# A hybrid attention block on one core: the weights' tiles begin 32 bytes lower, at a multiple of 256

## The chip, the cores and the metric

The kernel runs on one core of a Trainium2 chip, in one launch. Its time is the device time of one execution in microseconds (us), and a kernel's time is the median of its runs. A profile is one further execution, recorded by the hardware profiler; its times are the start and length of each instruction and of each DMA packet.

A core has a matrix engine (TensorE, "PE" in the profile, with its weight loads listed as "PEld"), a vector engine (VectorE, "DVE"), a scalar engine (ScalarE, "ACT"), GpSimd ("POOL"), and a sync engine ("SP") that issues DMAs. Operands lie in SBUF, a memory of 128 partitions; an address in this document is the byte within a partition, the same for all 128. A matrix product has a *stationary* operand, which a weight load puts into the array, and a *moving* operand, whose columns are streamed past it; in the kernel's calls these are `lhsT` and `rhs`.

## The reference, cut to what matters

Sixteen learned tokens are put before a sequence of 512 tokens of width 1024. One layer follows: a norm, one wide input projection (six blocks of 1024 columns), two branches of attention with eight heads each, gates, an output projection, and a gated feed-forward part (1024 to 2816 to 1024). All is float32.

```python
xn = rmsnorm(h, norm_mix_g[l])
proj = xn @ w_in[l]
sb_q, sb_k, sb_v, df_q, df_k, df_v = jnp.split(proj, splits, axis=-1)
...
y_sb = o_sb @ w_br_sb[l]
y_df = o_df @ w_br_df[l]
gates = jax.nn.sigmoid(xn @ w_gate[l] + b_gate[l]).reshape(B, L_pad, 2, D)
merged = gates[:, :, 0] * y_sb + gates[:, :, 1] * y_df
h = h + merged @ w_out[l]
hn = rmsnorm(h, norm_ffn_g[l])
h = h + (jax.nn.silu(hn @ w_ffn_gate[l]) * (hn @ w_ffn_up[l])) @ w_ffn_down[l]
```

## The kernel before, in words

**Products in three parts.** Each float32 operand is split into a rounded part (`h`, type float32r) and the remainder (`l`). `mm3` (lines 293 to 298) makes one product out of three matrix instructions per slice of 128 rows: line 296 takes h times h, line 297 the second pairing, line 298 the third. So nearly all of PE's work is on these three lines, 128 rows deep, with 256, 264 or 512 moving columns.

**The weights' way.** `stream` is the list of all 512 KB weight pieces in the order of use. `stage_one` (line 210 issues the DMA, on SP's queue) loads a piece from DRAM into a tile `wst`. `split` then makes `wh` on ACT (a copy with rounding, line 78) and `wl` on DVE (the difference, line 81). PE reads `wh` and `wl`. The tiles `wst` (three buffers), `wh` and `wl` (four each) are all those of the pool `wpool`, each 4,096 bytes per partition: 45,056 bytes in all. SP loads a buffer again when DVE has read it; ACT and DVE fill a buffer of `wh` or `wl` again when PE is done with it.

**Who is moving and who is stationary.** In the projections, the gates and the two feed-forward products (`proj`, `product`) a slice of `wh` or `wl` is stationary and the activations move: the normed input `xT` (tiles `xT_h`, `xT_l`, whole 512 tokens or the two halves `H1`, `H2` of 264), later the hidden state `hT` in the same places (halves `T1`, `T2` of 256 tokens), the attention output (`o_h`, `o_l`), and sums of blocks (`tA`, `tB`, and `t1`, `t2`, `t4`). In the output projection (`out_steps`) and the feed-forward's last product (`step`) it is the other way round: the activations (`mg_h`, `mg_l`, `t...`, and `da`) are stationary and `wh`, `wl` move, 512 columns at a time; only the last phase of `step` moves some in pieces of 256.

**Order.** The head of the program is written out by hand in order; behind it the units of one head's projection are woven into the attention of the one before. Each engine works through its own queue in program order and waits by semaphores.

**Where tiles lie.** Pools are laid out one after the other. First come the constants (pool `const`), with `cn` (two columns used, taken from a wider tile), `eps_c` and `var_max` as the last of them, all of these rounded up to 32 bytes; then `wpool`; then `xtp`, whose first tile is `pad_x`, used by nothing, followed by `xT_h` and `xT_l`; then the rest. In the program of the kernel before, the first `wst` begins at byte 20,000, the first `wh` at 32,288 and `xT_h` at 65,248. Within a block of 256 bytes these begin at 32, 32 and 224. All tiles of `wpool` begin at 32 (45,056 and 4,096 are multiples of 256), and so does each slice of 512 bytes of them. `xT` and `hT` begin at 224 in each of their rows; the second half `H2` of `xT` begins 1,056 bytes on, at 0; the 512 tokens behind the 16 learned ones begin 64 bytes on, at 32. The tiles `o_h`, `o_l`, `mg_h`, `mg_l` and `da` begin at 32, and `t1`, `t2`, `t4` at 224.

Of the kernel before, what the change touches and what calls it, by code (L numbers as in the profile page):

```python
# [9 lines left out]
F32 = mybir.dt.float32  # L10
# [6 lines left out]
P = 128  # L17
# [24 lines left out]
def block_kernel(ctx: ExitStack, tc: tile.TileContext, x, meta, norm_mix_g, w_in, w_gate, b_gate,  # L42
# [8 lines left out]
    const = ctx.enter_context(tc.tile_pool(name="const", bufs=1))  # L51
    wpool = ctx.enter_context(tc.tile_pool(name="wpool", bufs=4))
    xtp = ctx.enter_context(tc.tile_pool(name="xtp", bufs=1))
# [276 lines left out]

    xv = x[0].rearrange("(t p) d -> p t d", p=P)

    xtp.tile([P, 48], F32, name="pad_x")
    xT_h = xtp.tile([P, KT, XP], F32R, tag="xT_h", name="xT_h")
    xT_l = xtp.tile([P, KT, XP], F32R, tag="xT_l", name="xT_l")
    xT = (xT_h, xT_l)
# [473 lines left out]
        return [first, rest]  # L810

    g_sub = const.tile([P, 1], F32, name="g_sub")
    cn = const.tile([P, 16], F32, name="cn")[:, 0:2]
    csc, nlam = cn[:, 0:1], cn[:, 1:2]
    eps_c = const.tile([P, 1], F32, name="eps_c")
    var_max = const.tile([P, 1], F32, name="var_max")
# [176 lines left out]
    for br in range(2):  # L993
        name, head = (("y_sb", sb_head), ("y_df", df_head))[br]
# [536 lines left out]
```

## Time and profile before

| What | Value |
|---|---|
| median of 3 runs | 933.06 us (931.36 to 1141.8) |
| the profiled execution | 930.84 us, of which the span of the program's instructions is 929.1 us |
| PE | 916.9 us busy, 6,009 matrix instructions |
| DVE, ACT, POOL | 733.4, 583.6 and 168.6 us busy |
| DMA | 158.41 MB, 171 GB/s on average |

Busy time is time in which at least one instruction of the engine was in progress. Matrix instructions are pipelined: one begins before the one ahead of it has ended, so that the length shown for one (276 ns, say) is longer than the step from one start to the next. What PE delivers is read from the starts. A line of the kind "L296 PE MATMUL mm<-xT_h,wh" gives the code line, the engine, the operation, the tile that is written, and the moving and the stationary tile in this order.

### The profile page before, as it was taken

What the parts mean: (1) busy time and instruction counts of PE and PEld (TensorE: products, weight loads), DVE (VectorE), ACT (ScalarE), POOL (GpSimd) and SP (SyncE); (2) the same over time, 40 slices, a digit from 0 to 9 for tenths busy, and PEclk for the clock granted to TensorE, in tenths of its full rate; (3) what the DMA queues carried; (4) which work ended last, traced back from release to release, by engine and by line L of the source; (5) the groups of instructions that cost most, each with busy time, mean ns of one, the idle gap of its engine ahead of it and who ended that gap; (6) DMA issues with size and microseconds to landing.
All of it is one profiled execution on the core that took longest, in us unless ns stands there. A gap on an engine that the chain in (4) does not pass through costs nothing.

```text
span 929.1 us, 16027 instructions
## 1 busy us (share of the span) xinstructions
PE 916.9 (99%) x6009; PEld 835.0 (90%) x6010; DVE 733.4 (79%) x1412; ACT 583.6 (63%) x1102; POOL 168.6 (18%) x199
## 2 busy tenths in 40 slices
PE   8999999999999999999999999999999999999997
PEld 5999999998999899998988888899999999988886
DVE  7988877776677766976663787899888889799975
ACT  7665676676666666666665555775555655576554
POOL 4000121222333343344512000001100000000013
PEclk9999999999999999999999999999999999999999
DMA  8525788778777978799987774427754343276642
GB/s 253 143 72 161 167 185 199 177 167 252 192 191 175 220 168 182 183 208 192 194 207 175 220 262 159 126 79 182 172 129 120 93 135 92 92 271 194 191 148 91
DMA packets 155823, 158.41 MB, mean 171 GB/s; under 512 B 6465, under 2 KB 117218, under 8 KB 155746
## 3 DMA queue, kind: packets, MB, share of 16 engines
q1 hardware_dynamic: 132690, 101.61, 36.1%
q0 software_dynamic: 22896, 55.72, 29.3%
q8 instruction: 47, 0.77, 0.3%
q14 instruction: 30, 0.25, 0.1%
q10 hardware_dynamic: 160, 0.07, 0.0%
HBM read 133.64 MB, written 50.86 MB: 199 GB/s over the span
## 4 chain that ended last, share of the span: by engine, by line
PE 94%; DVE 2%; ACT 2%; issue 1%; DMA 0%; ACTq 0%; DVEq 0%
PE mm L296 22%; PE mm L297 22%; PE mm L298 22%; PE z L296 7%; PE z L298 7%; PE z L297 7%; PE z L563 2%; PE z L696 1%; PE z L695 1%; PE tr L537 1%; DVE wl L81 1%; PE z L584 1%; DMA wst<-in_w_ffn_up_dram 0%; DVE hres L1200 0%; PE mm L855 0%
## 5 line engine op out<-in xcount | busy, mean ns | idle before, releaser
L296 PE MATMUL mm<-xT_h,wh 128*128 128x264 f32 (+2 forms) x656 | 213.6, 326 | 0.5 <-ACT xT_h L898 0.5
L297 PE MATMUL mm<-xT_l,wh 128*128 128x264 f32 (+2 forms) x656 | 213.4, 325 | 0.5
L298 PE MATMUL mm<-xT_h,wl 128*128 128x264 f32 (+2 forms) x656 | 212.6, 324 | 0.0
L78 ACT CAST wh<-wst 128x1024 fp32r<-128x1024 f32 (+1 forms) x147 | 141.4, 966 | 77.4 <-PE mm L297 55.5
L81 DVE TENSOR_TENSOR wl<-wst,wh 128x1024 fp32r<-128x1024 f32 (+1 forms) x147 | 163.3, 1116 | 31.2 <-ACT wh L78 30.9
L297 PEld LDWEIGHTS mm<-xT_l,wh 128*128 128x128 f32 x656 | 123.4, 188 | 10.3 <-DVE xT_l L899 1.3
L298 PEld LDWEIGHTS mm<-xT_h,wl 128*128 128x128 f32 x656 | 123.5, 188 | 10.0
L296 PEld LDWEIGHTS mm<-xT_h,wh 128*128 128x128 f32 x656 | 123.4, 188 | 10.0 <-ACT xT_h L898 0.9
L296 PE MATMUL mm<-hT_h,wh 128*128 128x256 f32 x304 | 83.8, 277 | 0.9 <-ACT hT_h L1157 0.8
L298 PE MATMUL mm<-hT_h,wl 128*128 128x256 f32 x304 | 83.9, 277 | 0.0
L297 PE MATMUL mm<-hT_l,wh 128*128 128x256 f32 x304 | 83.8, 276 | 0.0
L296 PEld LDWEIGHTS mm<-hT_h,wh 128*128 128x128 f32 x304 | 56.9, 188 | 1.3 <-ACT hT_h L1157 1.0
L699 DVE CUSTOM_DVE_ANT_0 pr<-z,bias 128x144 f32<-128x144 f32 (+3 forms) x64 | 30.9, 502 | 34.0 <-PE z L696 31.8
L297 PEld LDWEIGHTS mm<-hT_l,wh 128*128 128x128 f32 x304 | 57.0, 188 | 0.0
L298 PEld LDWEIGHTS mm<-hT_h,wl 128*128 128x128 f32 x304 | 57.0, 188 | 0.0
L296 PE MATMUL mm<-o_h,wh 128*128 128x512 f32 x128 | 52.4, 410 | 0.0
L296 PE MATMUL z<-wh,da 128*128 128x512 f32 (+1 forms) x132 | 50.3, 381 | 0.0
L297 PE MATMUL z<-wl,da 128*128 128x512 f32 (+1 forms) x132 | 50.2, 381 | 0.0
L298 PE MATMUL z<-wh,da 128*128 128x512 f32 (+1 forms) x132 | 50.2, 380 | 0.0
L298 PE MATMUL mm<-o_h,wl 128*128 128x512 f32 x128 | 50.1, 391 | 0.0
L297 PE MATMUL mm<-o_l,wh 128*128 128x512 f32 x128 | 49.9, 390 | 0.0
L151 POOL DMA_DIRECT2D ds<-in_w_ffn_down_dram x36 | 30.2, 841 | 91.7 <-ACT wh L78 62.1
(359 smaller groups left out, 2464.5 us busy)
## 6 DMA issues: line engine op xcount, KB each, us to landing
wst<-in_w_in_dram SPq DMA_DIRECT2D x40, 512.0 KB, 6.3
ds<-in_w_ffn_down_dram POOLq DMA_DIRECT2D x30, 512.0 KB, 6.6
wst<-in_w_ffn_gate_dram SPq DMA_DIRECT2D x22, 512.0 KB, 4.0
wsu<-in_w_ffn_up_dram SPq DMA_DIRECT2D x20, 512.0 KB, 4.0
wst<-in_w_gate_dram SPq DMA_DIRECT2D x16, 512.0 KB, 4.8
y_df<-y_out POOLq DMA_DIRECT2D x32, 256.0 KB, 7.7
slots<-ds SPq DMA_DIRECT2D x13, 512.0 KB, 3.3
os<-in_w_out_dram POOLq DMA_DIRECT2D x12, 512.0 KB, 5.2
```

Of the source, the lines that this page charges most:

```text
L78: cast["last"] = (hi_copy or nc.scalar.copy)(hi, src)
L81: cast["lo"] = (lo_eng or nc.vector).tensor_tensor(lo, src, hi.bitcast(F32), op=ALU.subtract)
L151: tc.add_manual_dep(nc.gpsimd.dma_start(dst, src, **kw).ins, cast["last"].ins.name, paced)
L296: nc.tensor.matmul(ps, lhsT=ah, rhs=bh, start=(start and i == 0), stop=False, skip_group_check=skip)
L297: nc.tensor.matmul(ps, lhsT=ah, rhs=bl, start=False, stop=False, skip_group_check=skip)
L298: nc.tensor.matmul(ps, lhsT=al, rhs=bh, start=False, stop=(stop and i == n - 1), skip_group_check=skip)
L537: nc.tensor.transpose(pt[:, j * P:(j + 1) * P], vT[:, j * P:(j + 1) * P], ident)
L563: nc.tensor.transpose(pt[:, (t - j) * P:(t - j + 1) * P], blocks(t, j * P, (j + 1) * P), ident)
L584: nc.tensor.matmul(ps.rearrange("p (t q) -> p t q", q=P)[:, :, lo_rows:P], lhsT=vf[:, 1], rhs=a_s[:, 0:4 * qn], start=False, stop=True)
L695: nc.tensor.matmul(o, lhsT=q[c][:, qs], rhs=k[c][:, 0, k0:k1], start=True, stop=False)
L696: nc.tensor.matmul(o, lhsT=q[c][:, qs], rhs=k[c][:, 1, k0:k1], start=False, stop=True)
L699: nc.vector.tensor_tensor_reduce(po, zz, bb, scale=1.0, scalar=-3.0e38, op0=ALU.add, op1=ALU.max, accum_out=mx[:, t, c:c + 1])
```

## The change

`cn` is taken out of a tile of 8 columns (32 bytes) where it was 16 (64 bytes), and `pad_x` becomes 56 columns (224 bytes) where it was 48 (192 bytes). What is used of `cn`, and all instructions, stay as they are.

```diff
@@ -330,7 +330,7 @@
-    xtp.tile([P, 48], F32, name="pad_x")
+    xtp.tile([P, 56], F32, name="pad_x")
     xT_h = xtp.tile([P, KT, XP], F32R, tag="xT_h", name="xT_h")
@@ -810,7 +810,7 @@
     g_sub = const.tile([P, 1], F32, name="g_sub")
-    cn = const.tile([P, 16], F32, name="cn")[:, 0:2]
+    cn = const.tile([P, 8], F32, name="cn")[:, 0:2]
     csc, nlam = cn[:, 0:1], cn[:, 1:2]
     eps_c = const.tile([P, 1], F32, name="eps_c")
     var_max = const.tile([P, 1], F32, name="var_max")
```

Everything between the two tiles moves down by 32 bytes: all tiles of `wpool`, and with them the one-column constants `eps_c` and `var_max`. The tiles of `wpool` then begin at a multiple of 256. From `xT_h` on, addresses are what they were.

## The prediction

> **What bounds the kernel now.** I read the page first, then PE's waits, then single starts of matrix instructions in quiet stretches.
>
> ```profile
> span 929.1 us, 16027 instructions
> PE 916.9 (99%) x6009; PEld 835.0 (90%) x6010; DVE 733.4 (79%) x1412; ACT 583.6 (63%) x1102; POOL 168.6 (18%) x199
> PE 94%; DVE 2%; ACT 2%; issue 1%; DMA 0%; ACTq 0%; DVEq 0%
> ```
>
> The third line is the chain of work that ended last, by engine. PE holds 94% of it, and DMA rounds to nothing. The list of PE's waits is short:
>
> ```profile
> PE z L893 <- DVE xs L888: 1.4, 3, 0.7
> PE mm L855 <- DVE warm_w L848: 1.3, 1, 1.3
> PE mm L296 <- ACT hT_h L1157: 0.8, 1, 0.8
> PE mm L296 <- ACT xT_h L898: 0.5, 2, 0.2
> PE mm L296 <- ACT qy L1315: 0.5, 1, 0.5
> ```
>
> That is 4.5 us in all. So whatever the change does to the other engines is hidden behind PE, and the time moves as far as PE's step from one matrix instruction to the next moves. The change adds, removes and reorders nothing; it can act only through addresses. The question is whether PE's step knows them. The timeline shows starts; the first and the last row of six steps:
>
> ```profile
> 699.78 0.28 PE L298 MATMUL mm<-hT_h,wl 128*128 128x256 f32 x1
> 700.46 0.28 PE L298 MATMUL mm<-hT_h,wl 128*128 128x256 f32 x1
> ...
> 917.93 0.28 PE L298 MATMUL z<-wh,da 128*128 128x256 f32 x1
> 918.65 0.28 PE L298 MATMUL z<-wh,da 128*128 128x256 f32 x1
> ```
>
> Both are 256 columns of float32r without a wait. In the feed-forward's first products six steps take 0.68 us, 113.3 ns each; at the very end they take 0.72 us, 120.0 ns each. What differs is the tiles: in the first stretch the moving tile begins at byte 224 within 256 and the stationary one at 32, in the second both begin at 32. I write such a pair as 224/32. The same for 512 columns at 32/32, in a gate (moving `xT_h`) and in the last product (moving `wh`), six steps each:
>
> ```profile
> 529.73 0.39 PE L296 MATMUL mm<-xT_h,wh 128*128 128x512 f32 x1
> 531.09 0.39 PE L296 MATMUL mm<-xT_h,wh 128*128 128x512 f32 x1
> ...
> 849.81 0.39 PE L296 MATMUL z<-wh,da 128*128 128x512 f32 x1
> 851.17 0.39 PE L296 MATMUL z<-wh,da 128*128 128x512 f32 x1
> ```
>
> 1.36 us, 226.7 ns a step, twice the 113.3. And for 264 columns, the first half of `xT` at 224/32 and the second at 0/32, twelve steps each:
>
> ```profile
> 327.27 0.28 PE L296 MATMUL mm<-xT_h,wh 128*128 128x264 f32 x1
> 328.71 0.28 PE L296 MATMUL mm<-xT_h,wh 128*128 128x264 f32 x1
> ...
> 329.44 0.28 PE L296 MATMUL mm<-xT_h,wh 128*128 128x264 f32 x1
> 330.88 0.28 PE L296 MATMUL mm<-xT_h,wh 128*128 128x264 f32 x1
> ```
>
> 1.44 us both, 120.0 ns a step. So there is one place where a pair of phases seems to cost 6.7 ns a step, and several where it doesn't matter.
>
> **The change part by part.** How many instructions get which new pair; each row stands for the three lines L296 to L298:
>
> ```profile
> L296 PE MATMUL mm<-hT_h,wh 128*128 128x256 f32 x304 | 83.8, 277 | 0.9 <-ACT hT_h L1157 0.8
> L296 PE MATMUL mm<-t_h,wh 128*128 128x256 f32 x160 | 44.3, 277 | 0.5 <-ACT qy L1315 0.5
> L296 PE MATMUL z<-hT_h,wh 128*128 128x256 f32 x80 | 22.2, 278 | 0.0
> L296 PE MATMUL z<-t_h,wh 128*128 128x256 f32 x80 | 22.1, 276 | 0.0
> L296 PE MATMUL mm<-xT_h,wh 128*128 128x264 f32 x392 | 111.5, 284 | 0.0
> L296 PE MATMUL mm<-xT_h,wh 128*128 128x512 f32 x248 | 97.3, 392 | 0.0
> L296 PE MATMUL mm<-o_h,wh 128*128 128x512 f32 x128 | 52.4, 410 | 0.0
> L296 PE MATMUL z<-wh,da 128*128 128x512 f32 x121 | 47.2, 390 | 0.0
> L296 PE MATMUL mm<-wh,da 128*128 128x512 f32 x22 | 8.6, 389 | 0.0
> ```
>
> *Feed-forward, 256 columns*: 3 x (304 + 160 + 80 + 80) = 1,872 instructions go from 224/32 to 224/0. No row shows this pair. What it means is that the moving tile begins 32 bytes below the stationary one's block. The nearest row with that distance is the second half of `xT`, 0/32, and it steps as the first half does: 0 ns. The far end is the 6.7 ns of the equal pair: 1,872 x 6.7 = 12.5 us. I take 0, by the nearest row.
>
> *Projections, 264 columns*: 3 x 392 = 1,176. The first half goes to 224/0, as above: 0. The second, about 590, goes from 0/32 to 0/0, an equal pair. Equal pairs cost 6.7 ns at 256 columns and nothing that the 512-column rows show, so 0 to 590 x 6.7 = 4.0 us; I take the middle, 2.0.
>
> *512 columns, stationary weights*: 3 x (248 + 128) = 1,128 go from 32/32 to 32/0. The nearest row is one where the stationary tile lies at a multiple of 64 (`ones_r` begins at 192, its moving partner at 224, so the distance is 32 as well); beside it a row with another distance, 32/224, and its undisturbed sister in the same phase, 32/32:
>
> ```profile
> L758 PEld LDWEIGHTS tr<-sql,ones_r x8: 186/188/188, 285.6 to 485.6; 128*128 128x128 f32 x8
> L758 PE MATMUL tr<-sql,ones_r x8: 390/390/497, 285.9 to 485.6; 128*128 128x512 f32 x8
> ...
> L297 PE MATMUL mm<-wl,t_h 128*128 128x512 f32 x16 | 6.3, 394 | 0.0
> L297 PE MATMUL z<-wl,mg_h 128*128 128x512 f32 x8 | 3.1, 389 | 0.0
> ```
>
> 390 against 389 ns: a weights tile at a multiple of 64 loads no faster (188) and makes the instruction no shorter. The pair 32/224 costs 5 ns. So 0 to 1,128 x 5 = 5.6 us; by the nearer row, 1,128 x 1 ns = 1.1.
>
> *512 columns, moving weights*: 3 x (121 + 22) = 429 go from 32/32 to 0/32, a distance that cost nothing at 264: 0, at the far end 429 x 5 = 2.1 us. The 66 pieces of 256 columns at the very end (by the code, 11 slices times three instructions for each of two column halves, 120.0 ns a step) lose their equal pair: 66 x 6.7 = 0.4 us gained. The steps on `tA` and `tB` go through many distances, before as after, and those of the output projection are few: 0.
>
> *ACT, DVE and DMA* read and write the same tiles at the new phase.
>
> ```profile
> L81 DVE TENSOR_TENSOR wl<-wst,wh 128x1024 fp32r<-128x1024 f32 x118 | 144.0, 1222 | 31.0 <-ACT wh L78 30.7
> L78 ACT CAST wh<-wst 128x1024 fp32r<-128x1024 f32 x118 | 123.7, 1051 | 70.1 <-PE mm L297 55.5 <-PE z L298 8.9 <-ACT sg L785 2.2
> L81 DVE TENSOR_TENSOR wl<-wsu,wh 128x1024 fp32r<-128x1024 f32 x26 | 31.8, 1222 | 6.0 <-ACT wh L78 6.0
> wst<-in_w_in_dram SPq DMA_DIRECT2D x40, 512.0 KB, 6.3
> 597.32 4.27 DMA wst<-in_w_ffn_up_dram
> ```
>
> ACT's casts sat 55.5 us idle before PE freed a tile: they are ahead of PE. The difference on DVE takes 1222 ns whether its first input lies at 32 (`wst`) or at 224 (`wsu`), so I expect no other length at 0. Their cover is the four buffers; PE's only wait on them in the body is the 0.8 us for `hT_h`, behind the one landing on the chain (last row). A landing a third shorter or longer there moves 4.27 / 3 = 1.4 us: 0, and at most 1.4 either way. `eps_c` and `var_max` are single columns: 0.
>
> **Sum:** 0 + 2.0 + 1.1 + 0 - 0.4 + 0 = +2.7 us on the profiled execution's 930.84 us, 933.5. The median of the runs, 933.06, is 2.2 us above that execution, so the forecast is 933.06 + 2.7, about 936 us. With the ends of these terms and the 1.4 us of the loads it is -2 to +7, 931 to 940. From no change a measurement here can tell about 2%, 18.7 us: this is "within 2%".
>
> [...]
>
> **The rivals.**
>
> *Slower: the feed-forward's pairs turn costly.* The place is the 1,872 steps at 224/0, the price 6.7 ns each. It decides if what counts is not equality but that the two streams meet early, for then a 32-byte distance is nearly an equal pair. Alone it gives +12.5, with the 4.0 for the second half of `xT` 16.5, with the 5.6 and 2.1 of the 512-column steps 24: 946 to 957 us. Past 2% it goes only if nearly all of them pay. For it: the exact 6.7 ns. Against it: 0/32 at 264 columns, with the same distance, is free.
>
> *Faster: the present step carries a surcharge that aligned weights lose.* Four warm-up products in bfloat16, 512 columns each, show a shorter step:
>
> ```profile
> 8.47 1.03 PE L855 MATMUL mm<-warm,warm_w 128*128 128x512 bf16 x4
> L855 PE MATMUL mm<-warm,warm_w 128*128 128x512 bf16 x4 | 1.0, 379 | 0.0
> ```
>
> 1.03 us less the length of the last, 0.379, over three steps is 217 ns, 9.7 below 226.7. If each 512 columns lost 9.7 ns and each 256 or 264 half of it: (1,128 + 429) x 9.7 + (1,872 + 1,176) x 4.85 = 29.9 us, 903 us; half of that gives 918. For it: every weights tile of the trace but `ones_r` lies off a multiple of 64. Against it: `ones_r` at 390 ns, and 0/32, an aligned moving tile, which gains nothing.
>
> *Only the loads change.* The 512-byte pieces land in `wst` in whole blocks, and landings become shorter: at most 1.4 us at the one place above, 932 us. [...]
>
> **How the numbers follow.** The chances: forecast 0.60, loads only 0.08, slower 0.20, faster 0.12. The slower case lies on both sides of 951.7 (+2%); with the prices above it needs nearly all of them at once, but 6.7 ns is what one pair costs and bounds no other, so I put 0.13 of its 0.20 beyond. The faster case crosses 914.4 in a little over half: 0.07. So faster 0.07, within 2% 0.80, slower 0.13. The range leaves out about the lower two thirds of the faster case (0.08) and the upper half of the slower one (0.10): 920 to 953 us, with 936 as the time.
>
> **What would show it.** Step by step, in the profile of the changed kernel: starts in the feed-forward 113.3 ns apart (120 if the slower rival holds, 109 if the faster); in the second half of `xT` 120 to 127 ns; in the gates 226.7 to 228; at the very end 113 instead of 120; landings in `wst` near 6.3 us, or shorter for the third rival. I am wrong if PE's busy time moves by more than 10 us, or if PE waits for a `wh` that comes late.

## The result, and the profile after

| | before | after |
|---|---|---|
| median of the runs of one series | 935.91 us (931.36 to 1141.8, 6 runs) | 948.40 us (948.20 to 951.49, 6 runs) |
| ratio, 95% interval | | 1.0147 (1.011 to 1.0184) |
| the profiled execution | 930.84 us, span 929.1 | 948.33 us, span 946.6 |
| PE busy | 916.9 us | 935.2 us |

The changed kernel is slower by 1.5%. That lies within the 2% band, but well away from no change. One run of before, at 1141.8 us, stands far from all others; without it the median of before is 933.70 us (5 runs). Then 14.7 us lie between the medians, and 17.5 us between the two profiled executions. (Why these two differ is a finding of its own, below.)

The page after: span, busy times and the chain of waits by engine.

```profile
span 946.6 us, 16027 instructions
PE 935.2 (99%) x6009; PEld 843.6 (89%) x6010; DVE 735.8 (78%) x1412; ACT 584.7 (62%) x1102; POOL 168.3 (18%) x199
PE 93%; DVE 3%; ACT 2%; DMA 1%; issue 1%; SPq 0%; ACTq 0%; DVEq 0%
```

PE's busy time grew by 18.3 us and the span by 17.5; all other engines moved by 2.4 us or less (PE's own weight loads, PEld, by 8.6). PE's waits are as short as they were:

```profile
PE z L893 <- DVE xs L888: 1.3, 3, 0.7
PE mm L855 <- DVE warm_w L848: 1.2, 1, 1.2
PE mm L296 <- ACT xT_h L898: 0.5, 2, 0.2
```

So the loss is in PE's own steps. The timeline after shows the first and the last start of six steps, in turn for the feed-forward's first products, the very end, a gate and the last product; and of twelve steps for the second half of `xT`:

```profile
699.53 0.28 PE L296 MATMUL mm<-hT_h,wh 128*128 128x256 f32 x1
700.24 0.28 PE L296 MATMUL mm<-hT_h,wh 128*128 128x256 f32 x1
...
935.60 0.28 PE L296 MATMUL z<-wh,da 128*128 128x256 f32 x1
936.30 0.28 PE L296 MATMUL z<-wh,da 128*128 128x256 f32 x1
...
529.72 0.40 PE L296 MATMUL mm<-xT_h,wh 128*128 128x512 f32 x1
531.12 0.40 PE L296 MATMUL mm<-xT_h,wh 128*128 128x512 f32 x1
...
868.01 0.40 PE L296 MATMUL z<-wh,da 128*128 128x512 f32 x1
869.41 0.40 PE L296 MATMUL z<-wh,da 128*128 128x512 f32 x1
...
332.25 0.28 PE L296 MATMUL mm<-xT_h,wh 128*128 128x264 f32 x1
333.69 0.28 PE L296 MATMUL mm<-xT_h,wh 128*128 128x264 f32 x1
```

Feed-forward 0.71 us over six steps, 118.3 ns each, where it was 113.3. Gate and last product 1.40 us, 233.3 ns each, where they were 226.7. The very end 0.70 us, 116.7, a little less than its 120.0. The second half of `xT` 1.44 us over twelve, 120.0 as before. The rows by group (busy us and mean ns of one after the bar) say the same in lengths, which grew by about as much as the steps:

```profile
L296 PE MATMUL mm<-hT_h,wh 128*128 128x256 f32 x304 | 85.1, 282 | 0.0
L296 PE MATMUL mm<-t_h,wh 128*128 128x256 f32 x160 | 45.1, 282 | 0.5 <-ACT qy L1315 0.5
L296 PE MATMUL mm<-xT_h,wh 128*128 128x264 f32 x392 | 111.0, 283 | 0.0
L296 PE MATMUL mm<-xT_h,wh 128*128 128x512 f32 x248 | 98.5, 397 | 0.0
L296 PE MATMUL mm<-o_h,wh 128*128 128x512 f32 x128 | 53.2, 415 | 0.0
L296 PE MATMUL z<-wh,da 128*128 128x512 f32 x121 | 47.9, 395 | 0.0
```

Against before: 282 for 277, 282 for 277, 283 for 284, 397 for 392, 415 for 410, 395 for 390. Every group of 256 and of 512 columns shown here is 5 ns longer, and the one of 264 columns isn't.

The next table has the mean step of each group, worked out from the starts in the trace: from one start to the next, in stretches of at least six alike, steps over 300 ns (a wait) left out. It serves for the experiments too.

| group | steps | before | after | e1 | e2 | e3 | e4 | e5 |
|---|---|---|---|---|---|---|---|---|
| 256 columns, `hT` into `mm` | 909 | 114.0 | 118.9 | 113.8 | 120.3 | 118.8 | 114.6 | 114.5 |
| 256 columns, `hT` into `z` | 240 | 114.0 | 118.3 | 113.9 | 119.9 | 118.3 | 117.7 | 114.0 |
| 256 columns, sums `t` | 720 | 113.6 | 118.5 | 113.5 | 120.1 | 117.9 | 118.2 | 113.7 |
| 264 columns, `xT` | 1,176 | 121.2 | 120.7 | 121.1 | 122.3 | 120.7 | 120.9 | 121.3 |
| 512 columns, `xT` | 744 | 228.2 | 233.3 | 228.1 | 233.2 | 233.2 | 228.3 | 228.1 |
| 512 columns, `o` | 384 | 228.4 | 233.7 | 228.8 | 233.1 | 233.5 | 233.5 | 228.4 |
| 512 columns, weights moving, `da` | 426 | 226.9 | 233.3 | 226.9 | 229.0 | 233.3 | 233.3 | 227.0 |

Steps times difference, before to after: the 256-column groups 909 x 4.9 + 240 x 4.3 + 720 x 4.9 = 9.0 us; the 512-column groups 744 x 5.1 + 384 x 5.3 + 426 x 6.4 = 8.6 us; 264 columns -0.6 us. Three small groups are not in the table: `mg` stationary (94 steps, 226.7 to 233.1) 0.6 us, `t` stationary (72 steps, 229.0 to 233.3) 0.3 us, the very end (66 steps, 119.8 to 118.2) -0.1 us. Together that is 17.8 us against 17.5 us between the spans, so PE's steps are the whole of the loss.

Two more groups answer those on ACT and DVE, and two lines of the DMA issues (count, KB each, us from issue to landing) the one on the loads:

```profile
L81 DVE TENSOR_TENSOR wl<-wst,wh 128x1024 fp32r<-128x1024 f32 x118 | 143.9, 1221 | 34.0 <-ACT wh L78 33.7
L78 ACT CAST wh<-wst 128x1024 fp32r<-128x1024 f32 x118 | 123.7, 1050 | 74.0 <-PE mm L297 58.6 <-PE z L298 9.4 <-ACT sg L785 2.4
```

```profile
wst<-in_w_in_dram SPq DMA_DIRECT2D x40, 512.0 KB, 5.7
wst<-in_w_gate_dram SPq DMA_DIRECT2D x16, 512.0 KB, 5.3
```

1221 and 1050 ns against 1222 and 1051: the new phase of the tiles means nothing to DVE and ACT. Landings of the projections' weights are shorter, 5.7 against 6.3 us, those of the gates' longer, 5.3 against 4.8. Neither shows in the time, since PE's list of waits has no `wh` that came late.

### The profile page after: what moved, and what is told of

It reads as the page before. It is cut to its first block, busy times and chain, and to the rows that moved or that the text cites. A ratio compares the mean times of both kernels' runs of the same rounds, so it can differ in the third digit from the quotient of the medians.

```text
span 946.6 us, 16027 instructions
## 1 busy us (share of the span) xinstructions
PE 935.2 (99%) x6009; PEld 843.6 (89%) x6010; DVE 735.8 (78%) x1412; ACT 584.7 (62%) x1102; POOL 168.3 (18%) x199
## 4 chain that ended last, share of the span: by engine, by line
PE 93%; DVE 3%; ACT 2%; DMA 1%; issue 1%; SPq 0%; ACTq 0%; DVEq 0%
PE mm L296 22%; PE mm L297 22%; PE mm L298 22%; PE z L296 7%; PE z L298 7%; PE z L297 7%; PE z L563 2%; PE z L695 1%; PE z L696 1%; PE tr L537 1%; DMA lam<-in_lam_k_dram 1%; DVE wl L81 1%; PE z L584 1%; PE mm L855 0%; DVE hres L1200 0%
```

## The experiments

### One distance for all, at other addresses

Two theories are left when the steps are known to have grown. Either a tile at a multiple of 64 is dear in itself, or what counts is the distance between the moving and the stationary tile. `e1_all_lower` moves everything from the weights on by 32 bytes, the tiles behind them and those at the right end of SBUF too, so that all distances are those of before.

```diff
-    cn = const.tile([P, 16], F32, name="cn")[:, 0:2]
+    cn = const.tile([P, 8], F32, name="cn")[:, 0:2]
...
-    tsum = {n: tuple(tp.tile([P, 4, 256], F32R, name=f"{n}_{c}") for c in "hl") for n in ("t1", "t2", "t4")}
+    tsum = {n: tuple(tp.tile([P, 4, 256], F32R, name=f"{n}_{c}") for c in "hl") for n in ("t1", "t2", "t4")}; tp.tile([P, 8], F32, name="pad_t")
```

> Everything from the weights' tiles on lies 32 bytes lower than before: the weights at a multiple of 256 as after the change, but the activations with them, so that every distance between a moving and a stationary tile is that of before. Nothing else is changed. Theory D (the distance of the two operands' starts decides): steps as before, 113.3 ns for 256 columns and 226.7 ns for 512, ratio 1.000 to 1.004 against before. Theory M (an operand that begins at a multiple of 64 is dear in itself): all operands now begin at a multiple of 64, steps of at least 118 and 233 ns, ratio 1.013 or more.

Measured: 932.35 us (931.27 to 938.87, 10 runs), before 934.0; ratio 0.9977 (0.9944 to 1.0009). Two of its groups:

```profile
L296 PE MATMUL mm<-hT_h,wh 128*128 128x256 f32 x304 | 83.7, 277 | 0.7 <-ACT hT_h L1157 0.7
L296 PE MATMUL mm<-xT_h,wh 128*128 128x512 f32 x248 | 97.3, 392 | 0.0
```

277 and 392 ns, the lengths of before, with every weights tile at the very phase that it has in the changed kernel. The phase alone costs nothing; the distance decides.

### The weights at 96

If distances decide, the changed ones may be dear because they are odd multiples of 32, or because only the two distances of before are cheap. `e2_w96` puts the weights at 96 within 256 and leaves the rest: 256 columns then have a distance (moving start less stationary start, within 256) of 128, `xT` and `o` at 512 columns 192, the moving weights 64.

```diff
-    xtp.tile([P, 48], F32, name="pad_x")
+    xtp.tile([P, 32], F32, name="pad_x")
...
-    cn = const.tile([P, 16], F32, name="cn")[:, 0:2]
+    cn = const.tile([P, 32], F32, name="cn")[:, 0:2]
```

> The weights' tiles begin at 96 within 256 instead of 32, 64 bytes higher than before; the activations stay. No operand begins at a multiple of 64. Theory M: as before, 113.3 and 226.7 ns, ratio 1.00. Theory D in the form that distances of whole 64 bytes are cheap and those 32 off are dear: as before too. Theory D in the narrow form that 0 and 192 alone are cheap: the distances are now 128 for the feed-forward's 256 columns and 192 (or 64) for the 512 columns, so the 256-column steps are dear, 118 ns or more, ratio 1.008 to 1.015.

Measured: 948.92 us (948.27 to 950.5, 4 runs); ratio 1.0144 (1.0092 to 1.0196). Its groups:

```profile
L296 PE MATMUL mm<-xT_h,wh 128*128 128x512 f32 x248 | 98.5, 397 | 0.0
L296 PE MATMUL mm<-hT_h,wh 128*128 128x256 f32 x304 | 85.1, 282 | 0.3 <-ACT hT_h L1157 0.3
L296 PE MATMUL z<-wh,da 128*128 128x512 f32 x121 | 47.6, 393 | 0.0
```

As dear as the change, with distances that are multiples of 64. Each group has its own price: 120 ns at 256 columns and 128 apart, 233.2 at 512 columns and 192 apart, but only 229.0 at 512 columns and 64 apart (393 ns in the last row, between 390 and 395).

### The other operand moved

`e3_x_up` leaves the weights and moves what is behind them up by 32 bytes, which makes the same distances as the change, apart from the sums `t` at the right end.

```diff
-    xtp.tile([P, 48], F32, name="pad_x")
+    xtp.tile([P, 56], F32, name="pad_x")
```

> The weights' tiles stay at 32; all that lies behind them on the left side of the memory goes up by 32 bytes (the input and the hidden state to 0, attention output and the last product's stationary tiles to 64); the block sums t1, t2, t4 stay at 224. Theory D: the distances are 32 off again for all but the steps on t1, t2, t4 (480 of the 256-column steps), so 118 and 233 ns elsewhere, ratio 1.010 to 1.014. Theory M: the operands that moved are at a multiple of 64 and dear, which gives the same here, so this run tells only whether moving the other operand does the same as moving the weights. A theory that the weights' tiles alone matter (what ACT, DVE, DMA and weight loads do with them): ratio 1.00.

Measured: 947.6 us (947.1 to 949.25, 4 runs); ratio 1.0131 (1.0087 to 1.0174). The column e3 of the table is the column after, to 0.7 ns. Which of the two operands moves made no more difference than that. (The sums weren't moved by this edit, yet their steps are at 117.9. That was not expected; `b1_same` to `b3_same` and `p4_entry` below show that their distance, 192, has two paces.)

### The price of every distance

`p1_map` measures the step by itself: long stretches of matrix instructions on tiles `sta` to `sth` and `mva` to `mvh`, which begin at 0, 32, ... 224 within 256, where the code gives no other engine any work past the copies at its head.

> Not the block: a kernel of matrix instructions alone, nothing else running, that returns its input. float32r, one group for each of 8 x 8 pairs of start phases (0, 32, ... 224 within 256), 64 instructions of 256 columns and 32 of 512 columns; then six pairs with 128 to 448 columns, and the same pairs in bfloat16. Theory D (whole 64 bytes cheap): 113.3 and 226.7 ns wherever the phases differ by a multiple of 64, 118 and 233 otherwise. Theory M: dear wherever one of the two is 0, 64, 128 or 192. If the cause is another engine's traffic in the kernel, all pairs give the same here. bfloat16: about 217 ns for 512 columns at every pair if only four-byte operands collide.

In its timeline a row stands for several instructions ("x11"), with the time from the first start to the last end:

```profile
504.18 2.66 PE L54 MATMUL ps<-mva,sta 128*128 128x512 f32 x11
920.81 2.03 PE L54 MATMUL ps<-mvh,sta 128*128 128x512 f32 x8
21.74 1.48 PE L54 MATMUL ps<-mva,sta 128*128 128x256 f32 x11
381.78 1.41 PE L54 MATMUL ps<-mvg,sta 128*128 128x256 f32 x11
443.72 1.46 PE L54 MATMUL ps<-mvh,sta 128*128 128x256 f32 x11
1146.92 3.40 PE L54 MATMUL ps<-bmvh,bstb 128*128 128x512 bf16 x15
```

Less the length of the last (0.39 us at 512 columns, 0.28 at 256) and by one step fewer than instructions: 227 ns at distance 0 and 234 at 224 for 512 columns; 120 at 0, 113 at 192 and 118 at 224 for 256 columns. All 64 pairs, in ns a step, from the starts (eight pairs for each distance; a range where they differ by over 0.2):

| distance | 0 | 32 | 64 | 96 | 128 | 160 | 192 | 224 |
|---|---|---|---|---|---|---|---|---|
| 512 columns | 226.7 | 233.3 | 228.9 | 233.3 | 232.0 to 233.3 | 234.2 | 233.3 | 233.3 |
| 256 columns | 120.0 | 116.7 to 117.8 | 117.8 | 120.0 | 118.6 | 117.3 to 120.0 | 113.3 or 117.8 | 118.3 |

Pairs of the same distance agree wherever they lie, as in `e1_all_lower`, except where the table has a range: there one distance shows two values, most clearly 113.3 (three pairs) and 117.8 (five) at 192. The kernel's own numbers are here: the gates 226.7 at 0 and 233.3 at 32, the feed-forward 113.3 at 192 and 118.3 at 224, the `e2_w96` steps of 229.0 at 64. One is not: `e2_w96` had 120 at 256 columns and a distance of 128, where this table has 118.6; `p2_fine` below has 119.9 there. Other column counts, at six pairs: 128 and 192 columns 111.7 at all of them, 264 columns 120.0 to 122.2, which is why the projections' halves cared so little, 320 columns 146.7 at all, 384 columns 173.3 to 176.7, 448 columns 202.2 to 206.7. The same six pairs in bfloat16 all gave 109.2 and 215.8 at 256 and 512 columns (the last row: (3.40 - 0.38) / 14 = 215.7). Of the two types the distance counted for float32r alone.

No other engine has work here, so no other engine can be the cause: the 64 pairs differ by 3 to 6% with PE alone, 226.7 to 234.2 ns at 512 columns and 113.3 to 120.0 at 256. Whether the cause lies in what PE reads or elsewhere in PE, no run here tells. The bfloat16 steps, 109.2 and 215.8 ns, lie below every float32r step of these widths here.

### Finer distances, and a shorter stationary load

`p2_fine` steps the moving slice by 4 bytes from 0 to 256; `p3_load` makes the stationary tile 128, 96, 64 and 32 columns wide, at eight distances.

> Matrix instructions alone, the stationary tile fixed at a multiple of 256, the moving slice begun 0, 4, 8, ... 256 bytes above it, 40 instructions each, at 256 and at 512 columns; the kernel returns its input and leaves out the whole block. Theory D (the step is a function of the distance of the two starts within 256): the numbers of the coarse probe come back at 0, 32, ... 224 (512 columns: 226.7 at 0, 228.9 at 64, 233.3 at most others), the value at 256 is that of 0, and between two of these points the step stays near them. If the hardware counts in pieces of 32 or 64 bytes, the curve is a staircase of such pieces; if it counts in bytes, it slopes, and some distance between 0 and 32 or between 192 and 224 may be shorter than 226.7 or 113.3: a distance with 216 (the bfloat16 step) would be worth some 4% to this kernel.

Measured at 512 columns, ns a step for distances 0 to 60 by 4, from the starts:

```
226.7 236.7 233.4 228.9 231.8 236.0 233.3 226.7 233.4 234.7 233.4 230.0 233.4 233.3 233.3 226.7
```

No staircase, and no slope: neighbours 4 bytes apart differ by up to 10 ns. Over the whole range the steps lie from 226.7 (at 0, 28, 60, 108, 156 and 252) to 240.0, at 256 columns from 113.3 (at 16, 112, 144 and 192) to 123.4; none is near the bfloat16 step. The hope for some 4% falls: before, the 512-column steps of the kernel were already at 226.7 to 229.0 ns in the mean, beside the 226.7 that is the shortest seen.

> Matrix instructions alone, stationary tile of 128, 96, 64 and 32 columns at a multiple of 256, moving tile at each of the eight phases, 256 and 512 columns; the kernel leaves out the whole block. Theory W (the moving stream meets the weight load of the next instruction in what PE reads): with a quarter of the load the surcharge shrinks to about a quarter, 233.3 becomes 228.3 or less and 120.0 about 115. Rival R (the distance acts on the moving stream itself or on how an instruction starts, whatever the load's length): 233.3 and 120.0 stay as they are with 32 stationary columns. Both: at distance 0 and 512 columns 226.7 with 128 columns.

The first row is 128 stationary columns at distance 0, then 128 and 32 at distance 32:

```profile
54.74 2.43 PE L46 MATMUL ps<-mva,st 128*128 128x512 f32 x10
61.64 2.73 PE L46 MATMUL ps<-mvb,st 128*128 128x512 f32 x11
395.65 2.73 PE L46 MATMUL ps<-mvb,st 128*32 128x512 f32 x11
```

226.7 ns in the first, 234 in both others: here a quarter of the load leaves the surcharge whole, against theory W. At 256 columns it does not. The rows are 128 columns at distance 64, then 32 columns at distances 0 and 64:

```profile
20.81 4.87 PE L46 MATMUL ps<-mvc,st 128*128 128x256 f32 x40
345.85 4.71 PE L46 MATMUL ps<-mva,st 128*32 128x256 f32 x40
355.09 4.71 PE L46 MATMUL ps<-mvc,st 128*32 128x256 f32 x40
```

Less the last one's 0.28 us, over 39 steps, that is 118 ns with 128 columns and 114 with 32, at distance 0 too, where `p1_map` has 120.0 with 128. So the equal pair fell further than the 115 of theory W, against rival R. From the starts, the eight distances lie on average 4.6 ns above 113.3 with 128 columns and 2.4 with 32 (256 columns moving, the 120.0 of `p1_map` taken for distance 0 with 128), but 5.4 and 4.8 above 226.7 (512 columns moving). Neither theory holds at both widths. The cheap distances move as well: at 512 columns, distance 0 costs 231.7 with 32 stationary columns instead of 226.7, and with 96 the shortest step (226.7) is at distance 32. So the length of the load has a part in it, but the price does not simply scale with it. Where in PE the price arises stays open.

### One part of the change alone

`e4_act_down` makes the change and moves `xT`, `hT` and `tA` by the same 32 bytes; the rest keeps its place.

```diff
     tA = xtp.tile([P, 2, 2, 4, HL], F32R, tag="y_sb", name="tA")
+    xtp.tile([P, 8], F32, name="pad_y")
...
-    cn = const.tile([P, 16], F32, name="cn")[:, 0:2]
+    cn = const.tile([P, 8], F32, name="cn")[:, 0:2]
```

> Weights 32 bytes lower as in the change, and xT, hT and tA 32 bytes lower with them; everything behind keeps its address. So the steps on xT and hT get their old distance back, and those on o, mg, da and the sums t1, t2, t4 keep the new one. Theory D (each group pays its own distance, and the prices add): xT and hT held 8.2 of the 17.2 us by which the groups of steps grew, so 9.0 / 17.2 of the loss stays: 934 + 6.5 to 9.2, 940 to 943 us, gates again 226.7 ns a step, the first feed-forward steps on hT again 113.3, those on the sums 116 to 120. Rival (one place carries the loss, and the rest is hidden or moved): 934 or 948.

Measured: 941.74 us (939.49 to 942.98, 10 runs), before 938.09 in that series; ratio 1.0049 (1.0026 to 1.0072). Span 937.7, which is 8.6 above the 929.1 of the kernel before as first profiled, where 9.0 was worked out. Between the medians of this series only 3.7 us remain, as ten of its 13 runs of before lie at 937.6 or above. Its groups:

```profile
L296 PE MATMUL mm<-xT_h,wh 128*128 128x512 f32 x248 | 97.2, 392 | 0.0
L296 PE MATMUL mm<-o_h,wh 128*128 128x512 f32 x128 | 53.0, 414 | 0.0
L296 PE MATMUL mm<-hT_h,wh 128*128 128x256 f32 x304 | 84.0, 278 | 0.1
L296 PE MATMUL z<-hT_h,wh 128*128 128x256 f32 x80 | 22.5, 281 | 0.0
```

The gates are back (392), `o` isn't (414). Prices add, group by group. One row doesn't fit: `hT` into `z` has its old distance of 192 and stays at 281. Those steps come twelve at a time between twelve on the sums, which step at 117.8 here:

```profile
637.51 0.28 PE L296 MATMUL z<-hT_h,wh 128*128 128x256 f32 x1
638.93 0.28 PE L296 MATMUL mm<-t_h,wh 128*128 128x256 f32 x1
```

1.42 us over twelve, 118 ns at a distance that gives 113.3 elsewhere. `p1_map` had the same two values at 192. So at 192 there are two lasting paces. That what ran ahead chooses between them is the theory (L) that the next runs try.

### The kernel before, three times more

That would also explain why the kernel before spreads from 931 to 941 us, and the changed one only from 948 to 951.

> The kernel before, unchanged, profiled again: its runs spread from 931 to 941 us, those of the changed kernel only from 948 to 951. Theory L (at 256 columns and a distance of 192 the step has two paces, 113.3 and 117.8 ns, and it depends on what ran ahead which one holds): an execution above 935 us has a stretch of the feed-forward at 117.8 instead of 113.3 ns, up to 1,872 x 4.5 = 8.4 us, and every 512-column step as it was. Rival: the excess is waiting for loads or lies in the head, and every run of steps in the feed-forward keeps 113.3. An execution near 931 tells neither.

> As for the run ahead: another execution of the kernel before, unchanged. Theory L: above 935 us with feed-forward steps at 117.8 ns in a stretch. Rival: above 935 us with all of these steps at 113.3.

> As for the two runs ahead: a third execution of the kernel before, unchanged. Theory L: above 935 us with feed-forward steps at 117.8 ns in a stretch. Rival: above 935 us with all of these steps at 113.3.

Spans 938.3, 931.1 and 935.2 us. Groups of the first of them:

```profile
L296 PE MATMUL mm<-xT_h,wh 128*128 128x512 f32 x248 | 97.3, 392 | 0.0
L296 PE MATMUL mm<-hT_h,wh 128*128 128x256 f32 x304 | 84.9, 281 | 0.7 <-ACT hT_h L1157 0.5 <-ACT qx L1310 0.2
L296 PE MATMUL mm<-t_h,wh 128*128 128x256 f32 x160 | 45.0, 281 | 0.5 <-ACT qy L1315 0.5
```

The same program at the same addresses, and the feed-forward's groups are 281 ns long instead of 277, while the 512-column group is as it was. From the starts, in `b1_same` and `b3_same` alike: 117.0 for `hT` into `mm`, 117.4 into `z`, 117.3 for the sums; in `b2_same` 114.2, 114.4 and 113.9. That is 909 x 3.0 + 240 x 3.4 + 720 x 3.7 = 6.2 us above the execution profiled first, and `b3_same` is 6.1 above it. `b1_same` has 3.1 more; its gaps of over 300 ns add up to 29.1 us against 25.4 in `b3_same`. So theory L is right about the two paces: an execution of the kernel before that is caught in the longer one loses two thirds of what the change costs the feed-forward. That what ran ahead chooses is not shown: the instructions ahead are the same in all three executions. Nor do the distances ahead fix it alone: in `p1_map` the pairs `mvd`/`stf` and `mvc`/`ste` stand at 192 behind the same three distances, and one stepped at 117.8 and the other at 113.3. (One stretch ahead of `mvc`/`ste`, at distance 32, had itself run at 117.8 where the other's had 116.8.) The two paces also account for 14.7 us between the medians against 17.5 between the two profiled executions: the execution of before that was profiled first had the short pace, and of the five runs of before, 931.4 to 933.7 and 938.1 to 939.5 us, not all can have had it.

### Which lead brings which pace

> Matrix instructions alone: six steps at one distance as a lead, then 30 steps of 256 columns at another, for all 64 distances that are multiples of 4 bytes with three leads, and for 16, 112, 144 and 192 with 22 leads each; the kernel leaves out the whole block. Theory L (a distance has one or two lasting paces, and what ran ahead chooses): at 192 some leads end in 113.3 and others in 117.8 ns. A distance at which every lead ends in 113.3 would give the feed-forward of the kernel before its fast pace in all executions: 931 us in place of 931 to 941. Rival (the pace at 192 changes for a reason outside PE's own steps, such as another engine's traffic): with nothing else running, every lead at 192 gives the same pace.

Measured, as the mean of the last 16 of the 30 steps: at 192, 17 of 25 leads end in 113.3 and 8 in 117.8, with PE alone; the rival falls. Each lead ran once, so this doesn't tell a lead that chooses from chance. At 112 all 25 leads end in 113.3 (one mean was 114.1). At 16 and 144, which had shown 113.3 in `p2_fine`, nearly all end at 116.6 to 118.8. At the other distances the three leads all stay at 115.5 or more.

### A distance with one pace

`e5_112` is the kernel before with `hT` and the sums at 144 within 256, 112 above the weights.

```diff
-    tsum = {n: tuple(tp.tile([P, 4, 256], F32R, name=f"{n}_{c}") for c in "hl") for n in ("t1", "t2", "t4")}
+    tall = tp.tile([P, 24 + 6 * 1024], F32R, name="t_h")[:, 4:4 + 6 * 1024].rearrange("p (s k t) -> p s k t", s=6, k=4); tsum = {n: (tall[:, 2 * i], tall[:, 2 * i + 1]) for i, n in enumerate(("t1", "t2", "t4"))}
...
-    hT_h, hT_l = (xtp.tile([P, KT, SEQ], F32R, tag=t, name=n)
+    hT_h, hT_l = (xtp.tile([P, 44 + KT * SEQ], F32R, tag=t, name=n)[:, 44:].rearrange("p (k t) -> p k t", k=KT)
```

> The kernel before, with the weights where they were and only the moving operands of the 256-column steps moved: hT and the sums t1, t2, t4 begin at 144 within 256 instead of 224, 112 above the weights instead of 192 (the sums lie in one tile for that; the planner takes nine matrix instructions in another order at one place). At 112 every one of 25 leads in the probe ended in 113.3 ns, at 192 some ended in 117.8. Theory L: every execution has the feed-forward at 113.3, so the runs lie within 931 to 934 and the runs at 937 to 941 are gone; median 931 to 933, ratio to the kernel before (median 933 to 938) 0.993 to 0.999. Rival (the pace in the block is set by something the probe lacks, or activations written at this offset cost more): the runs spread to 941 as before, or are slower.

Measured: 933.6 us (931.11 to 935.43, 12 runs); before 934.11 (930.75 to 939.59, 17 runs); ratio 0.9983 (0.9962 to 1.0005). Of the 17 runs of before seven lie at 937.4 or above, of the 12 here none does. That is the effect that theory L forecast; the mean gains 1.4 us (933.5 against 934.9), and whether it is faster in the median the interval leaves open. Median and runs reach a little higher than the 931 to 933 and 934 expected. About 0.3 us of that is the 72 steps with `t` stationary, which this edit takes from 229.0 to 233.3. Its profile has the short pace all through the feed-forward:

```profile
L296 PE MATMUL z<-hT_h,wh 128*128 128x256 f32 x80 | 22.1, 277 | 0.0
L296 PE MATMUL z<-t_h,wh 128*128 128x256 f32 x80 | 22.0, 275 | 0.0
```

## Why the prediction was wrong in its terms

The measured 948.4 us lies in the range, 920 to 953, and the time moved less than 2%. But the sum said +2.7 us and the profiles say +17.5, and PE's busy time moved by 18.3 where 10 was named as the mark of being wrong. That the range holds the result is owed to the chance given to the slower rival and not to the sum, whose own bounds, 931 to 940, don't hold it. These bounds were not added up rightly either: the ends named with the terms give 4.0 + 5.6 + 2.1 - 0.4 + 1.4 = +12.7 us, and with the 12.5 of the feed-forward +25.2, where +7 was written. By its own steps:

- **PE alone sets the time, and the change acts only through addresses:** right. The steps of PE add up to 17.8 us, against 17.5 between the spans; ACT, DVE and the loads, taken at 0, gave nothing that shows.
- **Feed-forward, 256 columns, taken at 0:** the step that failed first. It measured 9.0 us. The row that it was taken from, the second half of `xT`, has the same distance of 224, but 264 columns, and at 264 columns the distance matters little (`p1_map`: 120.0 to 122.2). The row was near in distance and useless in shape. The far end of 12.5 us was a fair bound: 4.9 ns a step instead of 6.7.
- **264 columns, second half, taken at +2.0:** measured -0.6 for both halves. An equal pair costs next to nothing there (`p1_map`: 120.0 and 121.5).
- **512 columns, stationary weights, taken at 1.1:** measured 5.8, just past its far end of 5.6. Neither of the two rows quoted for it could give the price. `ones_r` at distance 32 showed 390 ns, but it stood as a pair of instructions between steps of other kinds, and the length of a lone instruction isn't a lasting step; alone and repeated, distance 32 gives 233.3. The row of `t_h`, sixteen instructions, showed 5 ns, near the 5.1 and 5.3 that were then measured, but by luck: it stands at distance 64, where the steps of this same trace are 229.0 (`p1_map`: 228.9), some 2 ns above the shortest; the 5 ns were read from the length of one of its three lines (392, 394 and 388 ns).
- **512 columns, moving weights, taken at 0:** measured 2.7 for `da`, past the far end of 2.1. The output projection, taken at 0 as its steps are few, added 0.6 (`mg`) and 0.3 (`t`). Again the 264-column row stood in for a shape that it doesn't speak for.
- **The very end, taken at -0.4:** -0.1. The mean of those steps went from 119.8 to 118.2 and not to 113: losing the equal pair is not the same as gaining the cheap one.
- **The slower rival:** the right place, at a chance of 0.20, and its 946 to 957 us holds the measured time. Its reason, that a small distance is nearly an equal pair, is not borne out: in `p2_fine` the step is 116.7 at 252 and 123.4 at 4 where the equal pair has 120.0, and at 512 columns the equal pair is the cheapest. Whether two streams meet at all is neither shown nor excluded. The faster rival falls: no distance gives a float32r step near the bfloat16 one (226.7 ns at the least against 215.8 at 512 columns, 113.3 against 109.2 at 256). Only the loads: that whole blocks land sooner was the author's guess, and no run shows it: the projections' weights landed sooner (5.7 us against 6.3), the gates' later (5.3 against 4.8), and neither shows in the time.
- **The median of before:** 933.06 of three runs became 935.91 of six, as runs at 938 and 939 came in. The prediction knew one pace of the feed-forward, the one of its profile; in the longer one the same term would have been 1,869 x 1.5 = 2.8 us (118.7 in the mean after, against 117.2).

Behind all of it stands one habit: the prediction sought a rule for the pair of phases ("equal is dear") in the few pairs that the trace happens to hold, at three shapes at once. Each shape has its own table. In `p1_map` the equal pair is the cheapest at 512 columns (226.7 of 226.7 to 234.2 ns), among the dearest at 256 (120.0 of 113.3 to 120.0), and at 264 there is little to choose (120.0 to 122.2).

## What to carry to other kernels

In these runs, with PE as the bound and float32r operands, the distance between the start of the moving and of the stationary tile within 256 bytes was worth 3 to 6% of a step at 256 and 512 columns (113.3 to 120.0 and 226.7 to 234.2 ns in `p1_map`), and 32 bytes in two tiles that no product reads cost 17.5 us between the two profiled executions. So after any change of the layout, read the steps from one start to the next and not the busy shares. A price seen at one column count said nothing for another (the change cost 4.3 to 4.9 ns a step in the groups of 256 columns, 5.1 to 6.4 in the three large ones of 512, and none at 264), and a lone instruction's length said nothing for a steady stretch (390 ns beside 389 for a pair at distance 32, which steps at 233.3 against 226.7 when repeated). When runs of one program spread and PE never waits, profile it several times and compare the groups: here the same step had two paces, 113.3 and 117.8 ns.

## What the runs showed of the hardware that was not expected

- The step of float32r products went by the distance and not by the absolute phase, the same to 0.2 ns at all eight phases except at the four places where the table of `p1_map` has a range: 226.7 to 234.2 ns at 512 columns by steps of 32 bytes, up to 240.0 by steps of 4 bytes (`p2_fine`); 113.3 to 120.0, and to 123.4, at 256. The values that recur (113.3, 120.0, 226.7, 233.3, 240.0) are 17, 18, 34, 35 and 36 times 6.67 ns.
- It happened with PE alone (`p1_map`), and not in bfloat16 (109.2 and 215.8 at all six pairs measured). With a stationary load of 32 columns instead of 128 (`p3_load`) the mean surcharge over eight distances fell from 4.6 to 2.4 ns at 256 columns, and only from 5.4 to 4.8 at 512.
- At 256 columns and a distance of 192 the same instructions have two lasting paces, 113.3 and 117.8, and the same program can run in either; what chooses is not shown. At a distance of 112 only the short one was seen, after 25 leads.
- Whether the cause lies in the reads from SBUF or inside PE, no run here tells.
